# Low parts of twelve weight tiles computed on VectorE, and SBUF tiles moved to multiples of 512 bytes, in a two-layer encoder trunk

## The chip, the cores and the metric

The kernel runs on one core of one Trainium2 chip. The metric is the device time of one execution in microseconds. Engines are named as in the profile: PE is TensorE's matrix multiply, PEld its weight load (each matmul has one, and it runs under the matmul before), DVE is VectorE, ACT is ScalarE, POOL is GpSimd, SP is SyncE, which only issues DMAs here.

## The reference

The program computes a trunk of two layers on a sequence of 512 frames of 1,024 features, in float32. Cut to what matters:

```python
for l in range(DEPTH):                                  # DEPTH = 2
    sh1, sc1, gt1, sh2, sc2, gt2 = split(silu(c) @ ada_w[l] + ada_b[l], 6)
    h = rms_norm(x, norm1_g[l]) * (1 + sc1) + sh1
    p = h @ w_in[l]                                     # 35 blocks of 128 columns
    br_gate = sigmoid(p[..., gates])                    # two gates of 1,024 columns
    y_a = rwkv7_time_mix(...)                           # a chunked recurrence, 8 heads
    y_b = multiscale_pool(...)
    mixed = br_gate[0] * (y_a @ proj_a[l]) + br_gate[1] * (y_b @ proj_b[l])
    x = x + gt1 * (mixed @ w_out[l])
    h2 = rms_norm(x, norm2_g[l]) * (1 + sc2) + sh2
    gate, up = split(h2 @ w_gu[l], 2)
    x = x + gt2 * ((silu(gate) * up) @ w_down[l])       # hidden width 2,816
return rms_norm(x, final_g)
```

## The kernel before

**Products in three passes.** Features lie on the 128 partitions, the 512 frames along them. A large product is done with both operands split into a high part (rounded to float32r) and a low part (the rest). `block` (L227) issues high weights by high data, high weights by low data, low weights by high data; each pass is one matmul with a 128x128 weight block and 512 (sometimes 256) columns of data.

**Weight tiles.** A tile of weights is 128x1024 float32, 4,096 bytes in each partition, eight 128x128 blocks of 512 bytes. `weights` (L179) takes the raw tile that `fetch` (L174) has loaded on SP's queue into one of three `raw` buffers, makes the high part with a cast on ACT (L195), and the low part in one of two ways that `self.by_dma` chooses. With `by_dma` set, ACT writes the negated raw tile as the low part (L198) and POOL issues a DMA that loads the same weights again from HBM and adds them into the tile (L199). Otherwise DVE subtracts (L201):

```python
        self.on(nc.scalar, "copy")(hi, raw)                                       # L195
        if self.by_dma and (self.by_dma is True or self.count % self.by_dma):
            nc.scalar.activation(lo, raw, AF.Copy, scale=-1.0)                    # L198
            nc.gpsimd.dma_start(lo, src, accum_op=ALU.add)                        # L199
        else:
            self.on(nc.vector, "tensor_tensor")(lo, raw, hi.bitcast(F32), ALU.subtract)   # L201
```

**The stages of a layer.** `mixer` (L1031) streams the blocks of `w_in`, computes the recurrence and the pooling, and streams the gate blocks under them; `by_dma` is on from L1064. In its last part (L1122 to L1126) the recurrence `chain` (L918) alternates with the generator `gates`, which ends with `side` (L512): the product with `proj_b`, each of whose eight results DVE multiplies (L533) with a gate tile that a DMA brings back (`g<-gd`). `side` also fetches the first two raw tiles of `proj_a`. Then comes a loop over m = 0..7 (L1137): twelve matmuls of `proj_a` with `ya` (the recurrence's result), then on DVE the product with the gate (L1150), the sum with `side`'s result (L1151), on ACT the high part `mh` (L245) and on DVE the low part `ml` (L246). The gate tiles have three buffers (`mg`, L1136), so the load for m is issued when the step m-3 has let its buffer go. At m = 5 and m = 7 the first two tiles of `w_out` are split. At L1159 `by_dma` goes off, and `product` (L1168) multiplies `mixed` with `w_out`; each of its results needs all eight `mh` and `ml`. `mlp` (L1342) then computes the hidden blocks, three directly and 19 by a seven-product scheme on halves of 256 columns (`seven`, L1286), and the product with `w_down` (`product`, L1488), 22 blocks for each of 8 outputs.

**Order.** The tile framework orders the instructions of each engine ahead of time by its own estimates, inside the dependencies of the tiles. While `self.pinned` is set, matmuls keep the program's order. Each engine, and each DMA queue, then runs its list in that order.

**Where tiles lie.** Pools stack from both ends of the partition: the left ones start behind the constants, the right ones (`side="right"`) come down from the top. A tile takes its size rounded up to 32 bytes. In the built program the constants begin at byte 16,512. Large tiles then lie at these offsets, modulo 512:

| tiles | offset modulo 512 |
|---|---|
| `raw`, `whi`, `wlo` of the pools `wraw` and `whl`; the data `hh`, `hl`; `x`, `kr`, `ar` | 96 |
| what follows `r4` in the temporary pools: `nt`, `nh`, the first raw tiles `wr`; `mh`, `ml`; weights of the pools `wo`, `wk` | 160 |
| everything at the right end: weights of the pool `third`, `yah`, `yal`, the hidden tiles (`f`, `fh`, `fl`), `th`, `tl`, `f11` to `f24`, `hf`, `row` | 480 |
| the small weights and data of `loras` (pools `sl` and `sm`) | 64 |
| the tiles of 2,080 bytes of the pool `pre` | multiples of 32 |

`r4` is a tile of 128x4 (16 bytes a partition) for the reciprocal norms, in the temporary pool in front of `nt`, with two buffers.

Of the kernel before, what the change touches and what calls it, by code (L numbers as in the profile page):

```python
# [12 lines left out]
F32 = mybir.dt.float32  # L13
# [4 lines left out]
DRAM = bass.MemoryType.DRAM  # L18

P = 128  # L20
D = 1024
S = 512
L = 2
KC = D // P
FF = 2816
FC = FF // P
NJ = 4
# [36 lines left out]

PARS = [(0, slice(0, C), slice(C, P)), (1, slice(C, P), slice(0, C))]

# [41 lines left out]
def constants():  # L108
    cst = np.zeros((P, N_CST), np.float32)
    p = np.arange(P)  # L110
    cst[:, 0:128] = np.eye(P)
    cst[:, 128:256] = (p[:, None] // C) == (p[None, :] // C)
    s, t = (p % C)[:, None], np.arange(C)[None, :]
    cst[:, 256:320] = s < t
    cst[:, 320:384] = s <= t
    cst[:, 384:896] = (np.arange(S) % C != 0)[None, :]
    for g, w in enumerate(WINDOWS):
        cst[:, 896 + 16 * g : 912 + 16 * g] = (1.0 / np.minimum(np.arange(1, 17), w))[None, :]
    return cst


class Trunk:
    def __init__(self, ctx, tc, a, out):
        self.ctx, self.tc, self.nc, self.a, self.out = ctx, tc, tc.nc, a, out
        self.pinned, self.last, self.by_dma = False, None, False
        self.third, self.turn, self.ahead, self.on_way, self.land = None, 0, 1, [], []
        self.count, self.fetched = 0, []
        self.hf, self.exact, self.later, self.keep = None, False, [], 0
        self.after = None
        nc = self.nc  # L130
        pool = lambda **k: ctx.enter_context(self.pool(**k))
        self.const = pool(name="const", bufs=1)
        self.wraw = pool(name="wraw", bufs=3)
        self.whl = pool(name="whl", bufs=2)
        self.hp = pool(name="hp", bufs=1)
        self.psum = pool(name="psum", bufs=4, space=PSUM)
        self.dram = pool(name="dram", bufs=1, space=DRAM)
        self.cst = self.const.tile([P, N_CST], F32, name="cst")
        self.cols = self.const.tile([P, N_COLS], F32, name="cols")
        self.ones = self.const.tile([P, P], F32, name="ones")  # L140
        self.mean = self.const.tile([P, 1], F32, name="mean")
        self.eps = self.const.tile([P, 2], F32, name="eps")
        self.mods = [self.const.tile([P, 48], F32, name=f"mods{l}") for l in range(L)]
        self.gsc = [self.const.tile([P, 16], F32, name=f"gsc{l}") for l in range(L)]
        self.omm = [self.const.tile([P, 15], F32, name=f"omm{l}") for l in range(L)]
        self.omka = [self.const.tile([P, 4], F32, name=f"omka{l}") for l in range(L)]
        self.xs = [self.dram.tile([P, S], F32, name=f"xs{k}") for k in range(KC)]
        self.yb = {
            (n, g): self.dram.tile([P, S], F32, name=f"{n}{g}") for n in ("yh", "yl") for g in range(4)
        }  # L150
        self.vf = [self.dram.tile([P, S], F32, name=f"vf{j}") for j in range(NJ)]
        self.hd = {k: self.dram.tile([P, S], F32, name=f"hd{k}") for k in AWAY}

    def pool(self, **k):
        if "space" in k:
            return self.tc.tile_pool(**k)
        return self.tc.tile_pool(reuse_waits="tile", **k)
# [136 lines left out]
    def head(self, w0):  # L294


        nc, a = self.nc, self.a
        self.cact = self.const.tile([P, D], F32, name="cact")
        nc.sync.dma_start(self.cact, a["c"].partition_broadcast(P))
# [6 lines left out]
        nc.gpsimd.memset(self.ones, 1.0)  # L306
        nc.gpsimd.memset(self.mean, 1.0 / D)
        nc.gpsimd.memset(self.eps[:, 0:1], EPS_RMS)
# [7 lines left out]

        raw = [w0.tile([P, D], F32, name=f"wr{i}", bufs=1) for i in range(KRV0)]
        cut = WHOLE * P
# [18 lines left out]
        def parts(i):  # L337
            if i == GV:
                ws.append((w0.tile([P, D], F32R, name=f"whi{i}", bufs=1), None))
                part = lambda t, at: t.rearrange("p (k n) -> p k n", n=P)[:, :, at : at + C]  # L340
# [3 lines left out]
            else:  # L344
                ws.append([w0.tile([P, D - cut], F32R, name=f"w{n}{i}", bufs=1) for n in ("hi", "lo")])
                self.split(*ws[-1], raw[i][:, cut:])
# [57 lines left out]
    def rstd(self, hs, between=lambda: None):  # L404

        nc = self.nc
        n = (hs.stop - hs.start) // P
        st = self.m()
        for w in range(n):
            at = hs.start + w * P  # L410
            self.mm(st[:, w : w + 1], self.ssum[:, at : at + P], self.mean, start=True, stop=True)
        r = self.tmp.tile([P, 4], F32, tag="r4", name="r4", bufs=2)
        nc.scalar.activation(r[:, 0:n], st[:, 0:n], AF.Sqrt, bias=self.eps[:, 0:1])
        nc.vector.reciprocal(r[:, 0:n], r[:, 0:n])
        dg = self.tmp.tile([P, S], F32, tag="sq", name="dg", bufs=2)
        for w in range(n):
            nc.vector.tensor_scalar(
                dg[:, w * P : (w + 1) * P], self.c("ident"), r[:, w : w + 1], None, ALU.mult
            )
        between()  # L420
        rb = st[:, 0 : n * P]
        self.mm(rb, self.ones, dg[:, 0 : n * P], start=True, stop=True)
        return rb

    def turned(self, hs, g):

        nc = self.nc
        n, half = (hs.stop - hs.start) // P, KC // 2
        st = self.m()
        r = self.tmp.tile([P, 4], F32, tag="r4", name="r4", bufs=2)  # L430
        out = self.hb[1].tile([P, n, D], F32, tag="hf1", name="y", bufs=1)
        both = [[self.acc() for i in range(2)] for w in range(n)]
        part = lambda t, w: t[:, hs.start + w * P : hs.start + w * P + P]
        turns = [(w, i * half + k) for i, w in ((0, 0), (0, 1), (1, 0), (1, 1)) for k in range(half)]
        nc.scalar.mul(self.x[-1][:, hs], self.x[-1][:, hs], g)
        for at, (w, k) in enumerate(turns):
            if at == 2 * half:
                for i in range(n):
                    self.mm(st[:, i : i + 1], part(self.ssum, i), self.mean, start=True, stop=True)
                nc.scalar.activation(r[:, 0:n], st[:, 0:n], AF.Sqrt, bias=self.eps[:, 0:1])  # L440
                nc.vector.reciprocal(r[:, 0:n], r[:, 0:n])
            i, k4 = divmod(k, half)
            self.mm(both[w][i][:, k4 * P : k4 * P + P], part(self.x[k], w), self.c("ident"), transpose=True)
        for w in range(n):
            for i, cs in enumerate((slice(0, S), slice(S, D))):
                if i:
                    nc.scalar.mul(out[:, w, cs], both[w][i], r[:, w : w + 1])
                else:
                    nc.vector.tensor_scalar(out[:, w, cs], both[w][i], r[:, w : w + 1], None, ALU.mult)
                (nc.scalar if i else nc.sync).dma_start(self.out[1][w * P : w * P + P, cs], out[:, w, cs])  # L450
# [580 lines left out]
    def mixer(self, l):  # L1031
        nc, tc = self.nc, self.tc
        right = ExitStack()
# [33 lines left out]
        with ExitStack() as ctx:  # L1067
# [53 lines left out]
            with self.pool(name="ch", bufs=1) as sc:  # L1121
                for step in self.chain(l, sc):  # L1122
                    self.go(gates, CHAIN[step])
            self.pinned = False
            proj = [self.weights(self.a["proj_a"][l, 0])]
            self.go(gates)  # L1126
        ya = [(self.ya[0][:, j, :], self.ya[1][:, j, :]) for j in range(NJ)]
# [539 lines left out]
```

## Time and profile before

| what | value |
|---|---|
| time before, median of 3 executions | 1476.82 us (1475.88 to 1486.47) |
| profiled execution: its time | 1479.65 us |
| profiled execution: its span | 1477.9 us |
| PE busy | 1429.7 us, 97% of the span |
| DVE busy | 1087.3 us, 74% |
| ACT busy | 751.0 us, 51% |
| POOL busy | 246.8 us, 17% |
| DMA | 299.28 MB, mean 203 GB/s |

All durations come from the one profiled execution. It lies 2.83 us above the median of the executions shown, and 1.75 us of its time lie outside its span. Busy time of PE is modelled: a matmul is entered with some 0.39 us although the next one starts 0.23 us later, so the pace of PE is read from start times, not from durations. A row of the timeline gives the start in us from the beginning of the span, the length in us, engine, line, operation, output and inputs, shapes, and how many instructions it merges; in brackets stands the idle time before and what ended it. In a row of groups, the figures are the total busy time and the mean length in ns, and behind the second bar the idle time.

### The profile page before, as it was taken

The numbers are of one execution on the slowest core, as the hardware profiler recorded it, in microseconds if no ns is written. First come the engines' busy times: TensorE is split into PE (matmuls) and PEld (weight loads), VectorE is DVE, ScalarE is ACT, GpSimd is POOL, SyncE is SP. The second block draws the span as 40 slices with busy tenths as digits, with TensorE's granted clock in tenths as the row PEclk, the third lists the DMA queues.
The fourth block names the chain that finished last, engine by engine and source line by source line (L and its number), as shares of the span: only waits on it lengthen the run. The fifth ranks groups of instructions, "written<-read, shape, count | busy, mean of one in ns | idle before, by whom it ended". The sixth has DMA issues, their size and how long they took to land. (4 is left out here: it accounts for less than half of the span.)

```text
span 1477.9 us, 25375 instructions
## 1 busy us (share of the span) xinstructions
PE 1429.7 (97%) x9982; PEld 1219.6 (83%) x9982; DVE 1087.3 (74%) x1846; ACT 751.0 (51%) x1031; POOL 246.8 (17%) x291
## 2 busy tenths in 40 slices
PE   5999998999999999999999999999999999999998
PEld 2767676777899999988897777877789999998887
DVE  7888958576788888876767685768578888887333
ACT  5576544344456656642336766443444656656221
POOL 0133321110022211100012334111102222110000
PEclk9999999999999999999999999999999999999999
DMA  8788689589839999778726747976974899885232
GB/s 319 235 268 238 193 227 254 148 261 271 236 101 230 234 215 226 179 251 287 260 87 180 181 113 168 261 176 191 289 235 131 208 219 223 192 187 169 87 100 71
DMA packets 112918, 299.28 MB, mean 203 GB/s; under 512 B 12128, under 2 KB 22624, under 8 KB 112800
## 3 DMA queue, kind: packets, MB, share of 16 engines
q1 hardware_dynamic: 90160, 227.93, 47.3%
q0 software_dynamic: 21776, 68.69, 25.5%
q8 instruction: 78, 1.28, 0.4%
q10 hardware_dynamic: 864, 1.05, 0.2%
q14 instruction: 40, 0.33, 0.1%
HBM read 269.84 MB, written 27.79 MB: 201 GB/s over the span
## 5 line engine op out<-in xcount | busy, mean ns | idle before, releaser
L221 PE MATMUL acc<-hh,whi 128*128 128x512 f32 (+1 forms) x1119 | 392.5, 357 | 0.2
L221 PE MATMUL acc<-hh,wlo 128*128 128x512 f32 (+1 forms) x1111 | 379.2, 346 | 8.3 <-DMA wlo<-in_w_in 7.5
L221 PE MATMUL acc<-hl,whi 128*128 128x512 f32 (+2 forms) x1119 | 369.3, 346 | 0.1
L195 ACT CAST whi<-raw 128x1024 fp32r<-128x1024 f32 x143 | 149.8, 1049 | 266.8 <-PE acc L221 175.2
L221 PEld LDWEIGHTS acc<-hh,wlo 128*128 128x128 f32 x1111 | 210.7, 190 | 36.7 <-DMA wlo<-in_w_in 9.2
L221 PEld LDWEIGHTS acc<-hh,whi 128*128 128x128 f32 x1119 | 212.1, 190 | 31.9 <-issue 2.4
L221 PEld LDWEIGHTS acc<-hl,whi 128*128 128x128 f32 (+1 forms) x1119 | 203.8, 189 | 26.4 <-issue 2.2
L201 DVE TENSOR_TENSOR wlo<-raw,whi 128x1024 fp32r<-128x1024 f32 x78 | 94.7, 1221 | 77.3 <-ACT whi L195 72.9
L221 PE MATMUL acc<-f,whi 128*128 128x512 f32 (+1 forms) x304 | 92.2, 386 | 0.0
L221 PE MATMUL m<-tl,f13h 128*128 128x256 f32 x304 | 86.0, 283 | 0.0
L221 PE MATMUL m<-th,f13l 128*128 128x256 f32 x304 | 86.0, 283 | 0.0
L221 PE MATMUL m<-th,f13h 128*128 128x256 f32 x304 | 85.9, 283 | 0.0
L241 ACT CAST f24h<-x 128x1024 fp32r<-128x1024 f32 x38 | 39.9, 1050 | 60.4 <-DVE x L241 60.4
L198 ACT ACTIVATE wlo<-raw 128x1024 fp32r<-128x1024 f32 x65 | 68.5, 1053 | 0.1
L221 PEld LDWEIGHTS acc<-f,whi 128*128 128x128 f32 x304 | 56.2, 188 | 12.3
L199 POOL DMA_DIRECT2D wlo<-in_w_in x41 | 35.9, 876 | 159.3 <-ACT wlo L198 159.3
L1283 POOL DMA_DIRECT2D f22l<-in_w_gu x38 | 32.8, 863 | 171.6 <-ACT f22l L241 164.4
L221 PE MATMUL acc<-f,wlo 128*128 128x512 f32 (+1 forms) x152 | 58.7, 386 | 0.0
L241 DVE TENSOR_TENSOR f24l<-x,f24h 128x1024 fp32r<-128x1024 f32 x38 | 46.5, 1224 | 16.3 <-ACT f24h L241 16.3
L221 PEld LDWEIGHTS m<-th,f13h 128*128 128x128 f32 x304 | 58.4, 192 | 0.0
L221 PEld LDWEIGHTS m<-th,f13l 128*128 128x128 f32 x304 | 58.4, 192 | 0.0
L221 PEld LDWEIGHTS m<-tl,f13h 128*128 128x128 f32 x304 | 58.2, 192 | 0.0
(338 smaller groups left out, 3434.0 us busy)
## 6 DMA issues: line engine op xcount, KB each, us to landing
raw<-in_w_in SPq DMA_DIRECT2D x63, 512.0 KB, 4.7
raw<-in_w_gu SPq DMA_DIRECT2D x50, 512.0 KB, 4.5
raw<-in_w_down SPq DMA_DIRECT2D x44, 512.0 KB, 3.5
wlo<-in_w_in POOLq DMA_DIRECT2D x41, 512.0 KB, 7.7
wlo<-in_w_gu POOLq DMA_DIRECT2D x40, 512.0 KB, 6.8
x<-in_w_gu SPq DMA_DIRECT2D x76, 256.0 KB, 4.4
row<-in_ada SPq DMA_DIRECT2D x30, 512.0 KB, 5.2
raw<-in_ada SPq DMA_DIRECT2D x25, 512.0 KB, 4.9
```

Of the source, the lines that this page charges most:

```text
L195: self.on(nc.scalar, "copy")(hi, raw)
L198: nc.scalar.activation(lo, raw, AF.Copy, scale=-1.0)
L199: nc.gpsimd.dma_start(lo, src, accum_op=ALU.add)
L201: self.on(nc.vector, "tensor_tensor")(lo, raw, hi.bitcast(F32), ALU.subtract)
L221: i = (tensor.transpose if transpose else tensor.matmul)(*args, **k).ins
L241: return (lambda *a, **k: self.tc.keep_in_program_order(op(*a, **k))) if self.exact else op
L1283: nc.gpsimd.dma_start(lo, two[:, b], accum_op=ALU.add)
```

## The change

Three edits, all of them below.

First, `by_dma` is switched off behind the recurrence, before the first tile of `proj_a` is split, and not only at L1159. In each layer this concerns the four tiles of `proj_a` and the first two of `w_out`, twelve tiles in all. Their low part is DVE's subtraction (L201) in place of ACT's negated copy and POOL's accumulating DMA.

Second, a tile `pad` of 88 floats (352 bytes a partition) is placed in the constants, and a pool `edge` with one tile of 120 floats (480 bytes) at the right end. Nothing reads or writes either.

Third, `r4` moves from the temporary pools to the constants, where its two buffers take 64 bytes.

What is left of the stack so moves up by 352 + 64 = 416 bytes, from 96 to 0 modulo 512; what stood behind `r4` moves by 416 - 64 = 352, from 160 to 0; what hangs at the right moves down by 480, from 480 to 0. The tiles of `sl` and `sm`, below the odd-sized pool `pre`, go from 64 to 96.

```diff
@@
 P = 128
+PADS = (88, 120)
@@ in Trunk.__init__
         self.omka = [self.const.tile([P, 4], F32, name=f"omka{l}") for l in range(L)]
+
+        self.const.tile([P, PADS[0]], F32, name="pad")
+        pool(name="edge", bufs=1, side="right").tile([P, PADS[1]], F32, name="edge")
@@ in rstd, and the same line in turned
-        r = self.tmp.tile([P, 4], F32, tag="r4", name="r4", bufs=2)
+        r = self.const.tile([P, 4], F32, tag="r4", name="r4", bufs=2)
@@ in mixer
                 for step in self.chain(l, sc):
                     self.go(gates, CHAIN[step])
             self.pinned = False
+            self.by_dma = False
             proj = [self.weights(self.a["proj_a"][l, 0])]
             self.go(gates)
```

More of the change, by code (lines that the diff above doesn't have):

```diff
@@ L429, in turned @@
         st = self.m()
-        r = self.tmp.tile([P, 4], F32, tag="r4", name="r4", bufs=2)
+        r = self.const.tile([P, 4], F32, tag="r4", name="r4", bufs=2)
         out = self.hb[1].tile([P, n, D], F32, tag="hf1", name="y", bufs=1)
```

## The prediction

> **What bounds the kernel now.** I read the page first, then the chain of waits, then the timeline of PE stretch by stretch, and last the waits around the twelve weight tiles.
>
> ```profile
> span 1477.9 us, 25375 instructions
> PE 1429.7 (97%) x9982; PEld 1219.6 (83%) x9982; DVE 1087.3 (74%) x1846; ACT 751.0 (51%) x1031; POOL 246.8 (17%) x291
> PE 35%; DMA 4%; issue 3%; DVE 3%; POOL 1%; ACT 1%; DVEq 0%; SPq 0%; POOLq 0%; ACTq 0%
> ```
>
> PE is entered as busy 97% of the span, and of what the chain explains by an engine most is PE. DMA has 4% of it, 59 us of 1477.9. So two things can move the time: the pace at which PE starts one matmul after another, and the few places where PE stands still. The change touches both.
>
> The pace is read from start times. Four stretches of plain three-pass matmuls of 512 columns, without stalls, then two of 256 columns:
>
> ```profile
> 932.38 0.39 PE L221 MATMUL acc<-hh,whi 128*128 128x512 f32 x1
> ...
> 943.27 0.40 PE L221 MATMUL acc<-hh,whi 128*128 128x512 f32 x1
> ...
> 948.86 0.39 PE L221 MATMUL acc<-hh,whi 128*128 128x512 f32 x1
> ...
> 1390.96 0.62 PE L221 MATMUL acc<-f,whi 128*128 128x512 f32 x2
> ...
> 1400.75 0.39 PE L221 MATMUL acc<-hh,whi 128*128 128x512 f32 x1
> ...
> 1406.20 0.62 PE L221 MATMUL acc<-f,whi 128*128 128x512 f32 x2
> ```
>
> ```profile
> 1201.91 0.28 PE L221 MATMUL m<-hh,f22h 128*128 128x256 f32 x1
> ...
> 1204.75 0.28 PE L221 MATMUL acc<-hh,whi 128*128 128x256 f32 x1
> ...
> 1206.19 0.28 PE L221 MATMUL m<-th,f13h 128*128 128x256 f32 x1
> ...
> 1210.51 0.28 PE L221 MATMUL acc<-hh,whi 128*128 128x256 f32 x1
> ```
>
> From 932.38 to 943.27 run two gate blocks of 24 matmuls with weights of the pool `whl`: data and weights both at 96 modulo 512; 10.89 us / 48 = 226.9 ns each. The next block has its weights in `third`, at 480: 5.59 / 24 = 232.9 ns. In `w_down`, 14 hidden tiles at 480 with weights at 96 take 9.79 / 42 = 233.1 ns, and the 8 hidden tiles in `hh`, at 96 like the weights, 5.45 / 24 = 227.1 ns. So in neighbouring stretches with the same work a matmul costs 6 ns more where its two operands begin at different offsets modulo 512. With 256 columns it goes the other way: 24 matmuls with data at 96 and weights at 480 take 2.84 / 24 = 118.3 ns, and 36 with both at 480 take 4.32 / 36 = 120.0 ns. Offsets of 96 and of 480 give the same pace as long as the two are equal; no stretch here has both at 0.
>
> **The change, part by part. Tiles at multiples of 512.** The change adds no instruction here; it gives nearly all weights and data the offset 0, so that every pair is an equal one. I counted the pairs by the tiles that the program's matmuls name: with 512 columns, 1,676 equal and 1,558 unequal; with 256 columns, 2,760 equal and 1,544 unequal. Of the 1,558, `w_down` has 588 (14 hidden tiles by three passes, for 7 outputs, in each of two layers): at 233.1 - 227.1 = 6.0 ns, 3.5 us. `w_in` and the first directly computed hidden blocks have 634, where weights lie in `third` or in a tile at 160: 634 x 6.0 = 3.8 us. `proj_a` has 96 (`yah`, `yal` at 480, weights at 96), 0.6 us. The last 240 are `w_out` (160 with 96), for which the rows above have no pair; between 0 and 6.0 ns I take 2, nearer to nothing since these offsets are only 64 apart: 0.5 us. Together 8.4 us saved. Against it, the 1,544 unequal ones of 256 columns lose 120.0 - 118.3 = 1.7 ns each, 2.6 us. Net -5.8 us. This lies on the path where PE is the bound, in `w_down` and the hidden blocks surely (no idle before those rows). In the gate stream PE sometimes waits for weights, and there a faster pace only makes the wait longer; if all 3.8 us go that way, -2.0 is left. From above, the bound is the floor of the first rival.
>
> **Transfers.** Every large landing tile begins at 96, 160 or 480 now, so no row shows an aligned one. The nearest are loads of the same 512 KB rows of `ada` into tiles at 96 (`raw`) and at 480 (`row`, `hf`):
>
> ```profile
> row<-in_ada SPq DMA_DIRECT2D x30, 512.0 KB, 5.2
> raw<-in_ada SPq DMA_DIRECT2D x25, 512.0 KB, 4.9
> ...
> hf<-in_ada SPq DMA_DIRECT2D x12, 512.0 KB, 4.5
> ...
> wlo<-in_proj_a POOLq DMA_DIRECT2D x8, 512.0 KB, 8.3
> ```
>
> Their medians are 5.2 and 4.5 us at 480 and 4.9 at 96, between the two: the offset doesn't order them. I take 0, and as bounds the spread of these medians about 4.85, 7% of the chain's 59 us either way, 4 us. [...]
>
> **The twelve low parts.** Removed: 12 negated copies on ACT, 12 accumulating DMAs on POOL, each a second read of 512 KB. Added: 12 subtractions on DVE.
>
> ```profile
> L201 DVE TENSOR_TENSOR wlo<-raw,whi 128x1024 fp32r<-128x1024 f32 x78 | 94.7, 1221 | 77.3 <-ACT whi L195 72.9
> 1066.21 0.50 PE L221 MATMUL acc<-yah,wlo 128*128 128x512 f32 x1 [1.02 <-DMA wlo<-in_proj_a]
> 1076.76 0.50 PE L221 MATMUL acc<-mh,whi 128*128 128x512 f32 x1 [0.43 <-ACT mh L245]
> 1077.49 0.51 PE L221 MATMUL acc<-ml,whi 128*128 128x512 f32 x1 [0.23 <-DVE ml L246]
> 1079.23 0.51 PE L221 MATMUL acc<-mh,wlo 128*128 128x512 f32 x1 [0.53 <-DMA wlo<-in_w_out]
> ```
>
> ACT gives up twelve copies and DVE takes 12 x 1.221 = 14.7 us. A low part now lands 8.3 us (median) after its issue; DVE has it 1.2 us after the high part, so the two stalls of the second layer that end with a `wlo` transfer, 1.02 + 0.53 = 1.55 us, go. What is late next is the chain of DVE and ACT for `ml`:
>
> ```profile
> 1066.52 0.69 DVE L1150 TENSOR_TENSOR g<-acc,g 128x512 f32<-128x512 f32 x1 [2.16 <-DMA g<-gd]
> 1067.24 0.69 DVE L1151 TENSOR_TENSOR g<-g,hh 128x512 f32<-128x512 f32 x1
> 1068.62 0.69 DVE L246 TENSOR_TENSOR ml<-g,mh 128x512 fp32r<-128x512 f32 x1 [0.69 <-ACT mh L245]
> 1069.23 0.68 DVE L1150 TENSOR_TENSOR g<-acc,g 128x512 f32<-128x512 f32 x1
> ```
>
> One m takes 1069.23 - 1066.52 = 2.71 us on DVE, as long as twelve matmuls on PE (12 x 0.227 = 2.72), and it is the last `mh` and `ml` that PE waits for at 1076.76 and 1077.49. DVE runs its list in order, so a subtraction put between these steps moves all later ones. In each m DVE idles 0.69 us, under ACT's `mh`; a subtraction put there costs 1.22 - 0.69 = 0.53, elsewhere 1.22. Three of the six per layer (the last of `proj_a`, two of `w_out`) fall in this loop: 1.6 to 3.7 us per layer. But the chain also starts late, because `g<-gd` came 2.16 us late through DMA engines that the accumulating transfers share:
>
> ```profile
> 1047.00:1077.00 30.00, 28.54 (x123) 22.69 (x122) 17.52 (x27) 12.92 (x18) 3.46 (x4) 1.00 0.97 254
> 1041.66 0.33 PE L221 MATMUL acc<-cst,yn 128*128 128x128 f32 x1 [1.62 <-DVE yn L1010]
> ```
>
> The DMA engines are 0.97 busy there; without six second reads of 512 KB a layer I expect `g` 1 to 2 us sooner, which about pays for the subtractions. The end of the recurrence is in the same position: PE waits 1.62 us for `yn` on DVE in the second layer, and the first two low parts of `proj_a` come onto DVE there, but also take an accumulating DMA away. Nothing waits for POOL's queue or ACT's freed time. The sum: -1.5 us. Bounds: all listed stalls gone (1.55 + 0.43 + 0.23 + 1.62 = 3.83), -4; six subtractions in the loops at 1.22 with nothing won, +7.3. I take the value nearest to the two transfer stalls, since those certainly go.
>
> **The pads and `r4`** issue nothing, and `r4` keeps its two buffers: 0. That the stacks now overlap by other bytes can add a wait for a closed pool's tile; the trace shows no price for one.
>
> **Sum.** 1479.65 - 5.8 - 1.5 = 1472.35 against the profiled execution, which lies 2.83 us above the median; so 1469.5, say 1470 us, 0.5% less. A change under 1% (14.8 us) is about what a measurement of this kernel cannot tell from none.
>
> **Rivals.** First, the remainder of the pace is itself a matter of the offset, and goes at 0. The raw products of the first blocks, in plain float32, show a floor:
>
> ```profile
> 27.27 2.74 PE L221 MATMUL acc<-nh,wr 128*128 128x512 f32 x6
> 29.84 2.74 PE L221 MATMUL m<-nh,wr 128*128 128x512 f32 x6
> ```
>
> (29.84 - 27.27) / 6 = 428 ns per record; if a record is two passes, 214 ns for 512 columns, 107 for 256. At that pace 3,234 x 13 ns and 4,304 x 13 ns go from the forecast, 42 + 56 = 98 us: 1372 us. Against it: equal pairs at 96 and at 480 have one and the same pace, so the common offset seems not to enter. [...] 5%.
>
> Second, the offset changes nothing that counts: PE takes the ns in other waits, or the pace at 0 is no better. Then only the low parts act: 1470 + 5.8 = 1476 us. For it: the gate stream has stalls that don't come from PE. 23%.
>
> Third, slower: at a common offset of 0 matmuls settle at the slow pace of the unequal pairs. Then the 1,676 equal ones pay 5.9 ns more (9.9 us), the 256-column ones 2.6 us, and with -1.5 the end is 1476.8 + 11.0 = 1488 us. It decides if rows of `hh,whi` with 512 columns stand 232 ns apart or more. Against it speak two offsets out of two. 8%.
>
> Fourth, DVE becomes the bound at the end of both mixers: +7.3 in place of -1.5 gives 1478 us. For it: the chain of 2.71 us a step has no slack. 14%.
>
> **Numbers.** The forecast, 1465 to 1475, has 50%. The range 1458 to 1481 takes in the second and fourth rival, the 4 us of the transfers and the -4 of the low parts; the first and most of the third lie outside. Faster by over 1% (under 1462): the first rival, and a forecast that gets the transfers and all stalls on top, 17% together. Slower by over 1% (over 1491.6): 6%, the third rival with something added or a new wait. The rest, 77%, within 1%.
>
> **What would show it.** Right: `f,whi` against `hh,whi` in `w_down` both at 227 ns, the block at 1201.91 at 120.0, no stall ended by a `wlo` of `proj_a` or `w_out`, `g<-gd` waits shorter. Wrong: paces unchanged or all at 232; a longer wait for `ml` or `yn` than before; landing medians of the `ada` rows down by more than 7%.

## The result and the profile after

The changed kernel takes 1466.97 us (median of 7 executions, 1466.23 to 1469.65) against 1475.88 us for the kernel before (7 executions beside it). The ratio is 0.9934, with a 95% interval of 0.9909 to 0.9958: 9 us less. The forecast was 1470 us, 0.5% less than before. The sign and the size of the sum were right; two of its terms were not, as will be seen.

First the page of the changed kernel, its span, its busy times and the engines in the chain that ended last:

```profile
span 1464.5 us, 25340 instructions
PE 1422.3 (97%) x9982; PEld 1223.3 (84%) x9982; DVE 1099.3 (75%) x1858; ACT 739.7 (51%) x1019; POOL 235.6 (16%) x279
PE 43%; DMA 1%; DVE 1%; issue 1%; ACT 0%; POOL 0%; DVEq 0%; SPq 0%; ACTq 0%; POOLq 0%
```

DMA has fallen from 4% to 1% of the chain. Twelve instructions have moved from ACT to DVE, and twelve have gone from POOL.

Next the timeline of PE at two of the places where the prediction read the pace, `w_down` with its 14 hidden tiles and the first of the 256-column stretches (start, length, instruction; the line L221 is now L225):

```profile
1378.96 0.62 PE L225 MATMUL acc<-f,whi 128*128 128x512 f32 x2
...
1388.48 0.39 PE L225 MATMUL acc<-hh,whi 128*128 128x512 f32 x1
...
1190.06 0.28 PE L225 MATMUL m<-hh,f22h 128*128 128x256 f32 x1
...
1192.94 0.28 PE L225 MATMUL acc<-hh,whi 128*128 128x256 f32 x1
```

The 42 matmuls of `w_down` take 9.52 / 42 = 226.7 ns each where they took 233.1, and the 24 of 256 columns 2.88 / 24 = 120.0 ns where they took 118.3. That is the prediction's first step, to the nanosecond.

Now the waits of PE around the ends of the two mixers, first of the kernel before, then of the changed one (engine, line, what it waited for; us in total, times, longest), one block for each layer:

```profile
PE m L221 <- DVE ssum L402: 1.2, 1, 1.2
PE acc L221 <- DVE yn L1010: 1.1, 1, 1.1
PE acc L221 <- DVE yal L1029: 0.9, 1, 0.9
PE acc L221 <- DMA wlo<-in_w_gu: 0.5, 1, 0.5
...
PE acc L221 <- DVE yn L1010: 1.6, 1, 1.6
PE acc L221 <- DMA wlo<-in_proj_a: 1.0, 1, 1.0
PE acc L221 <- DMA wlo<-in_w_out: 0.5, 1, 0.5
PE acc L221 <- ACT mh L245: 0.4, 1, 0.4
PE m L221 <- DVE ssum L402: 0.3, 1, 0.3
PE acc L221 <- DVE ml L246: 0.2, 1, 0.2
```

```profile
PE acc L225 <- DVE yn L1014: 0.4, 1, 0.4
...
PE acc L225 <- DVE yn L1014: 1.7, 1, 1.7
```

All that is left in the changed kernel is the wait for `yn`, which in the second layer is as long as before. Not only the two waits that end with a `wlo` have gone, which the prediction counted on, but also those for `yal`, `mh`, `ssum` and the first tile of `w_gu`, and in both layers.

DVE's timeline in the loop over m, second layer, changed kernel, shows where the subtractions went:

```profile
1051.45 0.69 DVE L250 TENSOR_TENSOR ml<-g,mh 128x512 fp32r<-128x512 f32 x1 [0.69 <-ACT mh L249]
1052.06 0.68 DVE L1155 TENSOR_TENSOR g<-acc,g 128x512 f32<-128x512 f32 x1
1052.66 1.22 DVE L205 TENSOR_TENSOR wlo<-raw,whi 128x1024 fp32r<-128x1024 f32 x1
1053.80 0.68 DVE L1156 TENSOR_TENSOR g<-g,hl 128x512 f32<-128x512 f32 x1
1054.45 0.69 DVE L1155 TENSOR_TENSOR g<-acc,g 128x512 f32<-128x512 f32 x1
1055.17 0.69 DVE L250 TENSOR_TENSOR ml<-g,mh 128x512 fp32r<-128x512 f32 x1
```

The planner put the next step's product (L1155 at 1054.45) ahead of this step's `ml`, into the 0.69 us in which DVE used to wait for ACT's `mh`. So a part of the subtraction is paid for out of idle time: in four of the eight steps of a layer DVE no longer waits for `mh`, in the second layer 2.7 us instead of 5.5, against 3.7 us for the three subtractions in the loop. No wait for `mh` or `ml` is left on PE.

Two more views, the issues of DMAs (median us from issue to landing) and the busy share of the DMA engines in a stretch like the prediction's 1047 to 1077 (the column before the last):

```profile
g<-gd SPq DMA_DIRECT2D x40, 256.0 KB, 6.0
raw<-in_w_out SPq DMA_DIRECT2D x16, 512.0 KB, 3.8
raw<-in_proj_a SPq DMA_DIRECT2D x8, 512.0 KB, 5.1
...
1035.00:1065.00 30.00, 30.00 (x134) 24.86 (x133) 25.02 (x38) 10.60 (x14) 0.00 (x0) 1.00 0.66 205
```

Before, the same three rows had 7.0, 5.1 and 8.2 us, and the share was 0.97. PE is busy through the whole of that stretch now.

**Where the 13 us of the two profiled executions went.** For each of the 9,982 matmuls I took the gap to the next start and subtracted the pace at equal offsets (227 ns, 120 ns). An excess up to 25 ns is counted as pace, a larger one as wait; what falls into a stretch at half the clock (below) is counted apart. Differences to the kernel before, in us, for the changed kernel and three of the experiments. Each column is one execution; a second one of the changed kernel had 2 us less in waits, so 2 us between two columns say little.

| | placement alone, at 0 | placement alone, at 160 | low parts alone | changed kernel |
|---|---|---|---|---|
| waits at the ends of the mixers (13.85 before) | +0.9 | -0.6 | -8.5 | -9.6 |
| all other waits | +2.5 | -0.5 | -0.7 | +0.7 |
| pace | -4.8 | -4.5 | +0.1 | -5.0 |
| stretches at half the clock (3.85 before) | +3.0 | +5.2 | -0.2 | +1.1 |
| sum | +1.5 | -0.3 | -9.3 | -12.8 |

### The profile page after: what moved, and what is told of

Read it like the earlier page. It is cut to its first block, busy times and chain, and to the rows that moved or that the text cites. A ratio compares the mean times of both kernels' runs of the same rounds, so it can differ in the third digit from the quotient of the medians.

```text
span 1464.5 us, 25340 instructions
## 1 busy us (share of the span) xinstructions
PE 1422.3 (97%) x9982; PEld 1223.3 (84%) x9982; DVE 1099.3 (75%) x1858; ACT 739.7 (51%) x1019; POOL 235.6 (16%) x279
## 5 line engine op out<-in xcount | busy, mean ns | idle before, releaser
L225 PE MATMUL acc<-hh,whi 128*128 128x512 f32 (+1 forms) x1119 | 393.3, 357 | 0.2
L225 PE MATMUL acc<-hh,wlo 128*128 128x512 f32 (+1 forms) x1111 | 379.8, 346 | 7.5 <-DMA wlo<-in_w_in 7.5
L225 PE MATMUL acc<-hl,whi 128*128 128x512 f32 (+2 forms) x1119 | 369.4, 347 | 0.1
L225 PEld LDWEIGHTS acc<-hh,wlo 128*128 128x128 f32 x1111 | 211.5, 190 | 34.6 <-DMA wlo<-in_w_in 9.1
L225 PEld LDWEIGHTS acc<-hh,whi 128*128 128x128 f32 x1119 | 213.1, 190 | 31.0 <-issue 2.4
L225 PEld LDWEIGHTS acc<-hl,whi 128*128 128x128 f32 (+1 forms) x1119 | 204.8, 190 | 25.5 <-issue 2.2
L205 DVE TENSOR_TENSOR wlo<-raw,whi 128x1024 fp32r<-128x1024 f32 x90 | 109.4, 1221 | 75.8 <-ACT whi L199 75.5
L225 PE MATMUL acc<-f,whi 128*128 128x512 f32 (+1 forms) x304 | 90.7, 381 | 0.0
L225 PE MATMUL m<-th,f13l 128*128 128x256 f32 x304 | 86.2, 283 | 0.0
L225 PE MATMUL m<-th,f13h 128*128 128x256 f32 x304 | 86.2, 283 | 0.0
L225 PE MATMUL m<-tl,f13h 128*128 128x256 f32 x304 | 86.2, 283 | 0.0
L225 PEld LDWEIGHTS acc<-f,whi 128*128 128x128 f32 x304 | 56.2, 188 | 10.8
L225 PEld LDWEIGHTS m<-th,f13h 128*128 128x128 f32 x304 | 58.4, 192 | 0.0
L225 PEld LDWEIGHTS m<-tl,f13h 128*128 128x128 f32 x304 | 58.4, 192 | 0.0
L225 PEld LDWEIGHTS m<-th,f13l 128*128 128x128 f32 x304 | 58.4, 192 | 0.0
L225 PE MATMUL acc<-f,wlo 128*128 128x512 f32 (+1 forms) x152 | 57.9, 381 | 0.0
L245 ACT ACTIVATE s<-s 128x512 f32<-128x512 f32 x38 | 24.0, 632 | 65.0 <-DVE s L245 65.0
```

The source lines that it names most:

```text
L225: i = (tensor.transpose if transpose else tensor.matmul)(*args, **k).ins
L245: return (lambda *a, **k: self.tc.keep_in_program_order(op(*a, **k))) if self.exact else op
```

## The experiments

**The two parts, each alone.** In the first kernel only `by_dma` is switched off, and no tile moves; in the second only the pads and `r4` are there.

```diff
             self.pinned = False
+            self.by_dma = False
             proj = [self.weights(self.a["proj_a"][l, 0])]
```

> The twelve low parts on DVE alone; all tiles stay where they were before, at 96, 160 and 480. Theory: the two effects add up; the profiled executions differ by 7.8 us in stalls of PE, nearly all around the ends of the two mixers, and by 5.0 us in pace, and the stalls belong to the low parts. Then this kernel lies 7 to 8 us under the kernel before (ratio about 0.995), and its paces are unchanged: 233 ns for w_down with its hidden tiles at 480, 118.3 ns for the 256-column products with unequal offsets. Rival (as the prediction priced it): the low parts bring only 1.5 us (ratio 0.999) and the other 6 us of stalls go because tiles at multiples of 512 let transfers land sooner.

Measured: 1470.13 us against 1478.52, ratio 0.9937 (0.9915 to 0.9959). The theory held: the low parts alone bring 9.3 us. They are the larger term, and the prediction had 1.5 us for them.

The second, as an edit of the changed kernel:

```diff
             self.pinned = False
-            self.by_dma = False
             proj = [self.weights(self.a["proj_a"][l, 0])]
```

> The tiles at multiples of 512 alone; low parts as before. Theory: only the pace changes, 8 us won on 512 columns and 3 lost on 256 columns: 5 us under the kernel before (ratio 0.9966), the stalls at the ends of the mixers (yal, wlo of proj_a and w_out, mh, ml, ssum) still there. Rival: the placement also takes the stalls away, 11 us under (ratio 0.9925). Second rival: a faster PE only waits longer; nothing won (1.000).

Measured: 1479.47 us against the same 1478.52, ratio 1.0005 (0.9990 to 1.0020). The second rival: nothing is won. And yet the trace has the pace as predicted, 4.8 us less over the kernel. The table shows what stands against it in the profiled execution: 3.4 us of waits, most of them away from the ends of the mixers, and 3.0 us of half clock more than in the kernel before. So the whole placement was tried once more in another layout, everything at 160 modulo 512 and the low parts as before:

```diff
-PADS = (88, 120)
+PADS = (0, 80)
...
-        self.const.tile([P, PADS[0]], F32, name="pad")
...
             self.pinned = False
-            self.by_dma = False
```

> The placement alone a second time, in another layout: every large tile at 160 modulo 512, low parts as before. Theory (with the accumulating reads still there, the 5 us won in pace come back as waits for transfers at the ends of the mixers, some 2.4 us, and as more stretches of 3.4 us at half the clock, some 2.5 us): ratio to before 0.998 to 1.002, mean granted clock about 0.993. Rival (the first placement run lost its gain by something particular to offset 0, or by chance): ratio 0.9965, the granted clock as in the kernel before, 0.9945.

Measured: 1476.23 us against 1477.54, ratio 0.9991 (0.9978 to 1.0003). The placement alone again brings nothing that stands clear of the measurement, and surely not its 5 us. Its profiled execution has 4.5 us less in pace, 1.1 us less in waits and 5.2 us more at half the clock.

**What half the clock is.** The placement run at 0 shows it best, in three stretches of 3.4 us that follow one another (their length, then busy us of PE, PEld, DVE, ACT and POOL with their counts, granted clock, DMA share, GB/s), and in PE's timeline:

```profile
1078.20:1081.60 3.40, 1.38 (x6) 0.84 (x5) 1.70 (x3) 1.05 (x1) 0.00 (x0) 1.00 0.74 189
1081.60:1085.00 3.40, 3.40 (x9) 2.64 (x8) 3.40 (x5) 0.63 (x1) 0.00 (x0) 0.50 0.69 231
1085.00:1088.40 3.40, 3.40 (x16) 2.81 (x15) 2.39 (x6) 0.62 (x1) 0.00 (x0) 1.00 0.89 269
```

```profile
1081.06 0.50 PE L225 MATMUL acc<-mh,wlo 128*128 128x512 f32 x1 [2.02 <-DMA wlo<-in_w_out]
...
1082.07 0.63 PE L225 MATMUL acc<-mh,wlo 128*128 128x512 f32 x1
1082.50 0.63 PE L225 MATMUL acc<-mh,whi 128*128 128x512 f32 x1
...
1085.04 0.39 PE L225 MATMUL acc<-mh,whi 128*128 128x512 f32 x1
1085.27 0.39 PE L225 MATMUL acc<-ml,whi 128*128 128x512 f32 x1
```

A wait of 2.02 us for `wlo` fills most of the stretch from 1078.20 to 1081.60; PE is busy for 1.38 of its 3.40 us. In the next 3.4 us the granted clock is 0.50 and matmuls start every 0.43 us; then they start every 0.23 us again. That costs 1.6 us more, after the wait is over. In the profiled execution of the kernel before the granted clock was 0.50 for 6.83 us from 160.37 and for 3.41 us from 225.22, in that of the changed kernel for 6.83 us from 160.50 and from 225.35, and in both for the last 5.4 or 5.5 us, in which PE had nothing left to do. In each of these two executions the first two starts are 64.85 us apart, 19.00 times 3.413. PE waited 3.57 us for `sig` and 3.13 us for `wlo` around these starts, in the changed kernel 3.89 and 2.86 us. In the 3.41 us ahead of them its records leave 1.29 and 2.69 us idle, in the changed kernel 1.32 and 2.00 us; but other stretches of the same grid with 1.44 to 1.74 us idle had a clock of 1.00 behind them, and the second half of the 6.83 us from 225.35 came after only 0.86 us idle. So these traces show no limit from which a wait brings half the clock. From 225.66 in the kernel before, seven matmuls took 3.08 us, 1.5 us more than at 0.227 us each. Costs of that size fit the spread of the kernel before, 1471.8 to 1486.5 us over all its executions here: among those beside each set of experiments, the time falls as the mean granted clock rises, with a correlation of -0.4 to -0.8.

So the wait of 2.02 us above was paid nearly twice, with 1.6 us behind it. The mean granted clock over all executions was 0.9927 with the placement alone at 0 (12 executions) against 0.9944 for the kernel before (17 of them): 0.0017 x 1479 = 2.5 us. At 160 it was 0.9945 against 0.9951, 0.9 us. For the layout at 0, the clock of all executions and the waits of the profiled one would account for the lost 5 us (-4.8 + 2.5 + 3.4 = +1.1 against +0.7 measured). At 160, the one profiled execution has no more waits than before, and some 3 us stay open, about as much as the interval of 1.9 us and the scatter of waits from one execution to the next leave room for. So it is measured twice that the placement alone brings no time that can be told from none; that waits take it is shown for one execution at 0 alone.

**Is 0 special, and what counts as equal?** Two variants of the changed kernel: all tiles at a common offset of 160; and the left tiles at 0, the right ones at 256.

```diff
-PADS = (88, 120)
+PADS = (0, 80)
...
-        self.const.tile([P, PADS[0]], F32, name="pad")
```

```diff
-PADS = (88, 120)
+PADS = (88, 56)
```

> The changed kernel, but with a common offset of 160 for the same tiles in place of 0 (no left pad, 320 bytes at the right). Theory: what counts is that data and weights begin at the same offset modulo 512, not that it is 0: the same time as the changed kernel (ratio to before 0.993), 227.0 and 120.0 ns everywhere. Rival: a multiple of 512 counts in itself, for the landing of transfers or for PE: slower than the changed kernel by up to 5 us (ratio 0.997).

> The changed kernel, but all that hangs at the right end begins at 256 modulo 512, the left tiles at 0: unequal pairs again, with a difference of 256. Theory (any difference modulo 512 costs as 384 did): about 1,318 matmuls of 512 columns pay 6 ns each, 1,544 of 256 columns win 1.8 ns: 5 us above the changed kernel (ratio to before 0.9965). Rival: offsets count modulo 256, so the pairs are equal: as the changed kernel (0.993). Second rival: half a period is the worst case; more than 6 ns each, more than 8 us above.

Measured beside the kernel before at 1478.52 us: 1465.41 us at 160, ratio 0.9907 (0.9884 to 0.9931), and 1465.81 us with 256 at the right, 0.9911 (0.9889 to 0.9934). A multiple of 512 has no value of its own that these times could show; what the paces show is the relation of the two operands (233.1 ns in the kernel before for 480 with 96, 226.9 and 227.1 for 96 with 96). And a difference of 256 ran like none, as `w_down` of the second kernel shows, with hidden tiles at 256 and weights at 0:

```profile
1380.39 0.62 PE L225 MATMUL acc<-f,whi 128*128 128x512 f32 x2
...
1389.91 0.39 PE L225 MATMUL acc<-hh,whi 128*128 128x512 f32 x1
```

9.52 / 42 = 226.7 ns, the pace of equal offsets. So the first rival of the second expectation held for this difference: taken modulo 256, the 384 of most pairs that the prediction called unequal, at 233.1 ns in `w_down`, is 128.

**Relief of the DMA engines, or a low part that is ready sooner?** The changed kernel beside three variants of it. First the kernel itself:

> The changed kernel itself, beside the next three on one chip. Theory (the two parts add up once the low parts are on DVE): ratio to before 0.991, between 0.988 and 0.9945, like the kernels with common offset 160 and with 256 at the right. Rival (the placement brings nothing in either case, and the low parts all): 0.9937 as the low parts alone.

Measured: 1467.14 us against 1477.91, ratio 0.9928 (0.9908 to 0.9947). Together with the two variants above and the first measurement, the four runs that have both parts and equal paces average 0.9920, against 0.9937 for the low parts alone: 2.5 us for the placement beside DVE's low parts, where intervals of 3 us on either side leave room for 0 and for 5.

Then DVE computes the low parts, and the twelve accumulating reads are issued all the same, into a spare tile (`again` makes it, 128x1024, and sets it to zero):

```diff
+            if self.spare is not None:
+                nc.gpsimd.dma_start(self.spare, src, accum_op=ALU.add)
...
             self.by_dma = False
+            self.again(ctx)
             proj = [self.weights(self.a["proj_a"][l, 0])]
+            self.spare = None
...
-            with self.pool(name="mg", bufs=3) as mg:
+            with ExitStack() as sx:
+                mg = sx.enter_context(self.pool(name="mg", bufs=3))
+                self.again(sx)
```

> The changed kernel with DVE's low parts, but POOL still issues the accumulating read of each of the twelve tiles, into a spare tile that nobody reads. Theory (the stalls went because the DMA engines carry six reads of 512 KB a layer less, so that gate tiles and raw tiles land sooner): most of the gain of the low parts goes, 5 to 8 us above the changed kernel, and the waits of DVE for g come back. Rival (the stalls went because the low part no longer takes the 8 us from issue to landing): within 2 us of the changed kernel.

Measured: 1481.88 us, ratio 1.0027 (1.0010 to 1.0043); 15 us above the changed kernel, and even above the kernel before. The reads alone undo more than the whole gain, though no result waits for them. Its waits in the second layer, of PE and of DVE, with two rows of DVE's timeline between them (lines are 6 to 10 further down than in the changed kernel), and the DMA share where DVE waits:

```profile
PE acc L231 <- DVE yn L1020: 3.8, 1, 3.8
PE acc L231 <- ACT mh L255: 1.0, 2, 0.5
...
1041.92 0.69 DVE L543 TENSOR_TENSOR hh<-acc,g 128x512 f32<-128x512 f32 x1 [5.41 <-DMA g<-gd]
1042.53 0.34 DVE L1020 TENSOR_SCALAR yn<-acc,mv 128x64 f32<-128x64 f32 x1
...
DVE hh L543 <- DMA g<-gd: 5.4, 1, 5.4
DVE g L1165 <- DMA g<-gd: 4.4, 1, 4.4
DVE hl L543 <- DMA g<-gd: 2.5, 1, 2.5
...
1040.00:1060.00 20.00, 17.08 (x69) 13.97 (x70) 14.03 (x22) 5.02 (x6) 4.27 (x5) 0.91 0.94 300
```

The same waits of DVE in the second layer of the kernel before:

```profile
DVE hl L533 <- DMA g<-gd: 8.6, 3, 4.4
...
DVE g L1150 <- DMA g<-gd: 2.2, 1, 2.2
...
DVE hh L533 <- DMA g<-gd: 1.6, 1, 1.6
```

DVE waits 5.4 + 4.4 + 2.5 = 12.3 us for gate tiles with the reads; in the kernel before it waits 12.4 us for them in this part, and in the changed kernel 5.4 us (2.7 for `hl`, 2.7 for `hh`). Over both layers it is 18.3 us before, 17.3 and 17.7 with the placement alone, 7.1 with the low parts alone, 6.6 in the changed kernel and 22.6 with the reads. While DVE waits, `yn` and `mh` behind it in its list wait too, and PE for them: `yn` runs at 1042.53, right behind the product that waited 5.41 us. The wait of 3.8 us on PE lies in a stretch whose granted clock is 0.91 on average over these 20 us, against 1.00 in the same stretch of the kernel before. So the twelve reads, and the gate tiles that land late behind them, are enough to undo the gain, although the low parts are ready early and ACT has its copies taken off. The run does not bring back each wait of the kernel before. Those that end with a `wlo` stay away, since DVE makes it; `yal` and `ssum` hardly wait either, while `yn`, `mh` and `ml` wait longer. For `yal` the gate tiles are not the reason that the profile shows: in the kernel before, the product ahead of it in DVE's list waited 3.13 us for PE. How the 9.3 us divide between the reads, the earlier low parts and the new order of DVE's list is not shown. The twelve reads go into one spare tile, and their medians from issue to landing are 8.5 us (`proj_a`) and 7.0 us (`w_out`), against 8.3 and 8.0 us in the kernel before; the run shows the direction, not the exact price of a read.

In proportion: `w_out`'s two tiles of each layer by DMA again, `proj_a`'s on DVE.

```diff
                     if m in (5, 7):
+                        self.by_dma = True
                         outs.append(wout(len(outs)))
+                        self.by_dma = False
```

> The changed kernel, but the two tiles of w_out in each layer get their low part by the accumulating DMA again; those of proj_a stay on DVE. Theory (relief of the DMA engines in proportion): a third of the gain of the low parts goes, 3 us above the changed kernel, with a wait for wlo of w_out of about 0.7 us in the second layer. Rival (the first two tiles of proj_a, which come while the recurrence ends, are what counts): within 1 us of the changed kernel.

Measured: 1469.67 us, ratio 0.9946 (0.9928 to 0.9964), 2.5 us above the changed kernel beside it. The waits at the ends of the mixers are 7.6 us against 5.4. That is the theory's third, though the two intervals overlap. The wait of 0.7 us for `wlo` of `w_out` that the theory named did not come; the longest that came back is one of 1.1 us for `ssum` in the first layer.

And further in the same direction, the four tiles of `proj_b` in each layer as well:

```diff
         self.pb = []
+        self.by_dma = False
         ws = [self.weights(self.a["proj_b"][l, 0])]
```

> The changed kernel, and the four tiles of proj_b in each layer also get their low part on DVE: eight accumulating reads of 512 KB less, 8 x 1.22 = 9.8 us more on DVE, during the recurrence. Theory (the DMA engines are the bound there too, their share is 0.96 to 1.03 in the stretches in which proj_b is multiplied): the wait for yn goes down from 1.7 us, and the time by 1 to 4 us (ratio 0.990). Rival (DVE carries the recurrence, and every subtraction delays yn by 1.2 us): 2 to 8 us slower than the changed kernel (0.9945 to 0.998).

Measured: 1465.46 us, ratio 0.9928 (0.9910 to 0.9946). At its place it does what the theory says: DVE waits for no gate tile any more, PE's wait for `yn` is gone in both layers and the waits at the ends of the mixers fall to 1.8 us, from 4.3 and 5.4 in the two executions of the changed kernel. In the time it doesn't show: the ratio is that of the changed kernel, 0.9928, with intervals of some 3 us on either side. The profiled execution had 6.0 us at half the clock, 1 more than those two, which covers a part of it at most. The rival, that DVE would be late, fell with these rows.

**Products of 256 columns.** Before, pairs with a difference of 128 ran at 118.5 ns and 380 pairs with data 64 below the weights at 117.0, both on average. Three of the seven products got other offsets by pads between their data tiles `t1`, `t3` and `t2`:

```diff
-        t = {i: tuple(pool.tile([P, half, S // 2], F32R, name=f"t{n}{i}") for n in "hl") for i in (1, 3, 2)}
+        t = {}
+        for i, n in ((1, 8), (3, 16), (2, 16)):
+            pool.tile([P, n], F32, name=f"pad{i}")
+            t[i] = tuple(pool.tile([P, half, S // 2], F32R, name=f"t{n}{i}") for n in "hl")
+        pool.tile([P, 88], F32, name="pad")
```

> The changed kernel with the data of three of the seven products of 256 columns moved by small pads: t1 to 32, t3 to 96, t2 to 160 modulo 256, their weights f13 and f24 still at 0; each product has 12 matmuls in each of 38 hidden blocks. Theory (a product of 256 columns is faster where its operands' offsets differ; before, a difference of 128 gave 118.5 ns, one of 192 gave 117.0 ns, one of 0 gave 120.0): each of the three runs at 117 to 119 ns, 1,368 x 2 ns = 2 to 4 us under the changed kernel. Rival (only some differences help): at 120.0 or above for some of the three; at least one price that tells which difference is best.

Measured: 1459.24 us, ratio 0.9879 (0.9858 to 0.9900), 8 us under the changed kernel beside it. The pace explains 2.0 us of it: differences of 32, 96 and 160 ran at 118.3, 119.2 and 118.7 ns on average. The mean granted clock of its 4 executions was 0.9960 against 0.9942, which is 2.6 us. Its one profile also has 2 to 4 us less in waits than the two of the changed kernel; why, isn't explained.

Then all three at 448, 64 below their weights, and the weights of the pool `wk` at 64 against data at 0:

```diff
+            ctx.enter_context(self.pool(name="wp", bufs=1)).tile([P, 16], F32, name="padw")
             wk = ctx.enter_context(self.pool(name="wk", bufs=4))
...
+        pool.tile([P, 112], F32, name="padt")
+        for i in (1, 3, 2):
+            t[i] = tuple(pool.tile([P, half, S // 2], F32R, name=f"t{n}{i}") for n in "hl")
+        pool.tile([P, 16], F32, name="pade")
```

> The changed kernel with the data of three of the seven products of 256 columns at 448 modulo 512 against weights at 0, and the weights of the pool wk at 64 against data at 0: the difference of -64 that ran at 117.0 ns before. Theory: 1,368 + 384 matmuls at 117 ns, 5.3 us under the changed kernel (ratio to before 0.9895 by pace alone), and faster than the differences of 32, 96 and 160, which gave 2.0 us of pace. Rival (the pace of a product hangs on more than the difference, so that these pairs run at 118 to 119 ns): 2 to 3 us under it.

Measured: 1455.93 us against 1477.54, ratio 0.9862 (0.9839 to 0.9886). It is the fastest kernel of the study. Three products in the second layer, 36 matmuls:

```profile
1185.64 0.29 PE L225 MATMUL m<-th,f13h 128*128 128x256 f32 x1
...
1189.73 0.28 PE L225 MATMUL acc<-hh,whi 128*128 128x256 f32 x1
```

4.09 / 36 = 113.6 ns, where the changed kernel has 120.0 and the theory had 117. Over the kernel, pace falls by 11.1 us. Last, the same difference for 2,952 pairs, by moving the weights `f13`, `f22`, `f24` and the pools `wo` and `wk` to 64 and leaving all data at 0, with the low parts of `proj_b` on DVE too:

```diff
...
+        if head:
+            pool.tile([P, 16], F32, name="padf", bufs=1)
         f[24] = tiles("f24", D, 2)
...
```

> The changed kernel, the low parts of proj_b on DVE too, and 2,952 instead of 1,752 products of 256 columns with data 64 below their weights modulo 512 (the factors f13, f22, f24 and the pools wo and wk at 64, all data at 0); 252 products of 512 columns in w_down get a difference of 64. Theory (114 ns at a difference of -64, as the last kernel's 1,748 ran; about 2.5 ns more for a 512-column product at 64; the waits at the ends of the mixers 2 to 3 us shorter): 1,200 x 6 ns - 252 x 2.5 ns + 2 = 8.5 us under the last kernel, ratio to before 0.980 to 0.982. Rival (the gain hangs on which side is moved, data or weights): about as the last kernel, 0.986.

Measured: 1460.44 us against 1476.32, ratio 0.9894 (0.9875 to 0.9912), slower than the last kernel by its median, though the two intervals just overlap. The same three products:

```profile
1189.32 0.28 PE L225 MATMUL m<-th,f13h 128*128 128x256 f32 x1
...
1193.56 0.28 PE L225 MATMUL acc<-hh,whi 128*128 128x256 f32 x1
```

4.24 / 36 = 117.8 ns with the same difference of 64. Over the kernel, 5.8 us of the last kernel's gain in pace are lost. The products of `w_down` with the hidden tiles at the right end, 252 of which have a difference of 64 now, took 2.3 us more in all than in the changed kernel.

So the difference alone doesn't set the pace. The pairs of `wk`, whose weights were moved in both kernels, show both paces within one kernel. In each layer 192 of them follow one another; here is the first layer of the fastest kernel:

```profile
401.07 0.28 PE L225 MATMUL acc<-hh,whi 128*128 128x256 f32 x1
...
403.31 0.28 PE L225 MATMUL acc<-hh,wlo 128*128 128x256 f32 x1
403.43 0.60 PE L225 MATMUL m<-dg,ones 128*128 128x256 f32 x2
...
405.70 0.28 PE L225 MATMUL acc<-hh,whi 128*128 128x256 f32 x1
...
407.06 0.28 PE L225 MATMUL acc<-hh,whi 128*128 128x256 f32 x1
```

Up to `m<-dg,ones` 19 matmuls take 2.24 us, 117.9 ns each; later 12 take 1.36 us, 113.3 ns each. The first 72 of each layer run at 117.8 ns and the other 120 at 113.3, which makes 115 on average, in both layers and in both kernels; the pace changes four matmuls behind `m<-dg,ones`, where the next weight tile begins. The pairs with the average of 117.0 in the kernel before do the reverse: 40 at some 113.5 ns, then 117.8 from where four `m<-mean,ssum` break the stream, in the middle of a weight tile. So at one difference there are two steady paces, 113.3 to 113.5 and 117.8 to 117.9 ns, and these streams went from one to the other at or near such a break. What decides which of the two comes stays open; that it matters which side is moved is not excluded.

## Why the prediction was right in sum, and wrong in two terms

**The pace** was right: 226.7 and 120.0 ns at offset 0, and -5.0 us over the kernel in the trace against the forecast's -5.8. The first rival (the remainder of the pace goes at 0) and the third (all at the slow pace) fell with the same rows. The first rival's 214 ns took a record of the plain float32 products for two passes, which no run shows; with all tiles at 0 these records still stand 428 ns apart, (29.73 - 27.16) / 6.

**That the pace becomes time** was too simple. The forecast took -5.8 in full and let only `w_in`'s 3.8 us be lost to waits. Alone the placement brings no time that can be told from none (ratios 1.0005 and 0.9991). In the profile at 0 this is the second rival's mechanism, PE taking the ns in other waits, and a second one that the prediction did not have, stretches at half the clock; at 160 most of the loss stays open. Beside DVE's low parts some 2.5 us of the 5 are seen, where the intervals allow anything from 0 to 5.

**The low parts** were mis-sized: -1.5, between -4 and +7.3, against -9.3 measured (-12.6 to -6.1). The step that failed is the bound "all listed stalls gone, 3.83, -4". The list held one layer's stalls, picked by whether their row named a low part or the loop over m. The waits for `yal` and `ssum` in the first layer, and for the first tile of `w_gu`, went with the low parts too, as the run of the low parts alone shows. What the twelve reads do was seen: on DMA engines that are 0.97 busy, gate and raw tiles land 1 to 3 us later behind them (medians of 7.0, 5.1 and 8.2 us against 6.0, 3.9 and 5.3 with the low parts alone), and DVE waits 18.3 us for gate tiles instead of 7.1. Which of the single waits on PE hang on that is shown for `yn` alone. All waits from the end of the recurrence to the first hidden blocks came to 13.85 us in the two layers, and that sum was the bound to take. The prediction did see the share of 0.97 and expected `g` 1 to 2 us sooner (7.0 to 6.0 us), but spent it on DVE's subtractions. These left no wait on PE, as the planner put a part of them into the 0.69 us under `mh`; so the fourth rival fell too.

**The transfers**: 0 for the alignment of landing tiles was right. Common offsets of 0 and 160 give times that can't be told apart (ratios 0.9934 and 0.9928 at 0, 0.9907 at 160, the intervals overlapping), and the medians of the `ada` rows went from 5.2 to 4.8 (`row`), from 4.9 to 5.1 (`raw`) and from 4.5 to 4.4 us (`hf`), in no one direction. `row` by itself passes the 7% that the prediction had named as a sign of being wrong, but it is at 5.0 in the second execution of the changed kernel. The time of a single packet of 4,096 bytes on SP's queue has a median of 159 ns in the kernel before, in the changed one and with all tiles at 160.

So 1470 against 1466.97 came from a term too large by some 3 to 6 us and one too small by 8. That the two errors nearly cancel is luck. The remark that a change under 1% can't be told from none was too careful: the interval here is 0.25% on either side.

## What to carry to other kernels

Where the DMA engines are near 1.0 busy (0.97 here), price a transfer by every wait that ends late in that stretch, not by the waits that carry its name; issuing it without using it is the experiment that tells whether the transfer itself costs, though not which wait it causes. Where matmuls are back to back, look at both operands' start addresses modulo 256: it costs pads of some bytes, and here 512 columns ran at 226.7 ns with a difference of 0 or 256 against 233.1 with 384, while with 256 columns unequal was better than equal (113.3 to 119.2 ns against 120.0). Then measure the time too, since the 5 us in pace alone brought none here. And read the granted clock in windows of 3.4 us before comparing two executions that differ by a few us: half the clock came to 3.85 us in one profiled execution here and to 9.05 us in another.

## What was not expected of the hardware

- A pair of data and weights whose start offsets differ by 256 ran at 226.7 ns for 512 columns, like an equal pair; one with a difference of 384, which is 128 modulo 256, at 233.1 ns.
- With 256 columns, pairs with a difference of -64 ran at 113.3 or at 117.8 ns, both steady (120 and 72 matmuls of one layer of the fastest kernel), against 120.0 at equal offsets; within one stream the pace switched at or near a break by a few other matmuls.
- A wait of 2.02 us on PE was followed by 3.4 us at a granted clock of 0.50, which cost 1.6 us more; the five profiled executions of the table, the kernel before among them, had 3.65 to 9.05 us of such costs.
